# Moving the first head's load and two differential steps ahead of the end of the local units, with a fetch of local outputs moved forward

## The chip, the cores and the metric

The kernel runs on one core of one Trainium2 chip, in one launch. The metric is the device time of one execution in microseconds, taken as the median of several executions. The engines are named as in the profile: PE (TensorE), DVE (VectorE), ACT (ScalarE), POOL (GpSimd), SP (SyncE, which here only issues DMAs).

## The reference

One encoder layer with 1024 tokens and 16 meta tokens ahead of them, model width 1024, everything in float32. What is computed, cut to what matters here:

```python
h = h + 0.5 * swiglu(rmsnorm(h), ...)            # FFN 1
z = rmsnorm(h) @ w_in                            # one projection, columns split in groups
# group A: differential attention, 4 heads, 2 components of 64 dims each, full length 1040
s = einsum('bqhcd,bkhcd->bhcqk', q, k) * scale
p = softmax(s)
a = p[:, :, 0] - lam * p[:, :, 1]
A = rmsnorm(einsum('bhqk,bkhe->bqhe', a, v)) * (1 - lambda_init)
# group B: window attention +-128 tokens, 8 query heads on 2 key heads, a sink logit per head
B = softmax_with_sink(q . k in the band and the meta tokens) @ v
h = h + concat(A, rmsnorm(B)) @ w_out
h = h + 0.5 * swiglu(rmsnorm(h), ...)            # FFN 2
return rmsnorm(h)
```

## The kernel before, in words

Every product that needs float32 accuracy is made of several passes over numbers that are split in a high part (a rounding, on ACT) and a low part (the subtraction, L114). The layer runs in stages: FFN 1, the projections, attention, the output projection, FFN 2. The order of the instructions of each engine is settled at build time by a scheduler that simulates the program; each engine then takes its own instructions strictly in that order, and SP takes its DMA issues in order as well.

**Projections and local units.** The projections (`pj`, L167, and `pv`) go through DRAM: their outputs `z` get a rotary step (a product `zs` on POOL, two additions on DVE, L851) and are written to `qa_d`, `ka_d` (differential queries and keys), `qb_d`, `kb_d` (local ones). Beside them run the 16 *local units*, one for each of 2 key heads and 8 blocks of 128 queries. A unit consists of `win_keys`, `win_scores` (four products `ws`, for each a masked minimum on DVE, L1044, and an exponential on ACT, L1060; then `es`, `rz`, and four scalings on POOL, L1068) and `win_values` (four transposes `wt` for each key block, split in `thi` on ACT and `tlo` on DVE, and two products for each block into one accumulator `wo`, L1095; the result goes over `otmp` and `ow` to `ow_d`). The probabilities of a unit live in a ring `p4` of 4 buffers. `wo`, `otmp` and `ow` have one buffer each, so a unit's first `wo` product waits until DVE has added up the unit before.

The generator `fillers` is drawn from inside the local units: `qb_pair`, then `ka_pair`/`qa_pair` twice (the last projections), then `early_steps`, which loads the first differential head and makes the first N_EARLY of the differential steps.

**Differential steps.** There are 32 of them (4 heads, 8 query tiles). One step has two *score products* `ds` (components 0 and 1, six matmuls each, L780), for each a row minimum `dmx` on DVE (L784) and an exponential `dp` on ACT (L786), then `combine` (a reciprocal on DVE, L791, a scaling on POOL, L793, and a sum of both on DVE, L794). The combined tile is transposed (`wt` in the early steps, `dt` in the loop) and copied to `at` by DVE (L808) and ACT (L810, L814) two steps later. For each pair of steps `values` (L1228) multiplies with `v` and ACT copies the result to `oh`. Score products are counted below as S(step).(component), from S0.0 to S31.1.

**Loading a head.** `load_head` (L745) fetches `kraw` and `qraw` of a component with SP from `ka_d` and `qa_d`, ACT casts them to `kh` and `qst` and POOL subtracts for `kl` (L114) and for the lower half of `qst` (L760). `kraw` and `qraw` have one buffer each.

**The loop and its side work.** The main loop (L1243) starts at step N_EARLY = 4. `win_norm` is called at i = 4 and 8: it loads half of the local outputs from `ow_d` into `own` (L1171, one buffer), ACT and POOL make the sum of squares (L1148, L1151, L1152), PE sums over partitions (L1154), and POOL, ACT and DVE scale and split (L1174 to L1177) into `ow_hi`, `ow_lo`. From i = 9 on, odd steps draw from `out_fill`: the local half of the output projection (`out_win`, L1207, twelve matmuls `do<-ow_hi/ow_lo` for each of 16 pieces). What is left of it after the loop is run behind the loop.

## Time and profile before

| | us |
|---|---|
| three runs | 2072.01, 2071.40, 2064.84 |
| median | 2071.4 |
| the profiled execution: its own time | 2065.43 |
| its span in the trace | 2063.7 |
| last projection's matmul starts | 979.4 |
| last local product `wo` starts | 1061.0 |
| first product of the output projection starts | 1122.5 |
| S15.1, the 32nd score product, starts | 1159.9 |

Over the whole span PE is busy 94%, DVE 62%, ACT 43%, POOL 46%. The stage that the change touches lies between 979.4 and 1159.9 us. A row of the timeline gives start, busy time, engine, line, names and, in brackets, the idle time that lay just before it with the instruction that ended it. Starts of successive matmuls say more about PE than its busy time, since matmuls overlap.

### The profile page before, as it was taken

To read this page: it belongs to the slowest core of one execution; us is meant where nothing else is said; L and a number is where in the kernel's file an instruction comes from. 1 tells how busy PE (TensorE), PEld (TensorE's weight loads), DVE (VectorE), ACT (ScalarE), POOL (GpSimd) and SP (SyncE) were. 2 spreads that over 40 slices of the span, in tenths; PEclk is the share of its full clock that TensorE was granted. 3 is DMA by queue.
4 is the path that set the end of the run, shared out by engine and by line. 5 is a ranking of instruction groups with operands and counts; after the bars stand their busy time and mean duration, and the time that the engine had idled before them with its cause. 6 is when DMAs were issued, how large, how long until landed. Compare 5 with 4: busy or idle time off the path is not lost.

```text
span 2063.7 us, 30320 instructions
## 1 busy us (share of the span) xinstructions
PE 1942.7 (94%) x11484; PEld 1686.3 (82%) x11484; DVE 1281.4 (62%) x1857; ACT 880.0 (43%) x1630; POOL 950.8 (46%) x807
## 2 busy tenths in 40 slices
PE   5999999999999999999787999998999999989998
PEld 4999999998999889888555777676888888867777
DVE  7855555547874670277877777477655545587745
ACT  6433333334442441365766666353333333334433
POOL 0555554545443750666635433004655454454443
PEclk8999999999999999999898999999999999999999
DMA  4232323228522341533613322523323323475222
GB/s 173 99 118 99 119 83 109 88 100 314 169 70 77 127 147 62 132 104 80 152 49 87 98 67 72 179 92 96 123 103 113 107 77 123 147 265 164 62 82 82
DMA packets 104275, 237.82 MB, mean 115 GB/s; under 512 B 14016, under 2 KB 28816, under 8 KB 104128
## 3 DMA queue, kind: packets, MB, share of 16 engines
q1 hardware_dynamic: 92608, 198.20, 30.7%
q0 software_dynamic: 11520, 37.67, 4.7%
q8 instruction: 90, 1.47, 0.3%
q14 instruction: 57, 0.47, 0.1%
HBM read 169.86 MB, written 65.44 MB: 114 GB/s over the span
## 4 chain that ended last, share of the span: by engine, by line
PE 73%; DVE 11%; ACT 5%; DMA 5%; POOL 3%; issue 3%; SPq 1%; DVEq 0%; POOLq 0%; ACTq 0%
PE p L226 39%; PE pA L577 8%; PE pj L167 4%; PE pC L577 4%; PE pv L936 3%; PE do L1228 2%; PE pd L167 2%; PE ds L780 2%; PE po L167 2%; PE pB L577 2%; DVE bl L114 2%; PE do L167 1%; PE wo L1095 1%; ACT dp L786 1%; DMA wdraw<-wd 1%
## 5 line engine op out<-in xcount | busy, mean ns | idle before, releaser
L114 POOL TENSOR_TENSOR s<-ru 128x512 f32<-128x512 f32 x42 | 55.6, 1323 | 258.1 <-DMA ru<-wu 189.5
L226 PE MATMUL p<-b_hi,wal 128*128 128x260 f32 (+1 forms) x528 | 142.2, 324 | 5.1 <-DVE wal L114 5.1
L226 PE MATMUL p<-t_hi,wch 128*128 128x260 f32 (+1 forms) x528 | 140.8, 321 | 6.5 <-DVE u L114 6.5
L226 PE MATMUL p<-b_hi,wah 128*128 128x260 f32 (+1 forms) x528 | 143.6, 326 | 3.4 <-ACT sg L252 1.9
L226 PE MATMUL p<-b_lo,wah 128*128 128x260 f32 (+1 forms) x528 | 143.3, 324 | 3.3 <-DVE b_lo L114 3.3
L226 PE MATMUL p<-t_lo,wch 128*128 128x260 f32 (+1 forms) x528 | 140.6, 320 | 0.0
L226 PE MATMUL p<-t_hi,wcl 128*128 128x260 f32 (+1 forms) x528 | 140.2, 320 | 0.0
L226 PE MATMUL p<-t_lo,wbh 128*128 128x260 f32 (+1 forms) x504 | 135.9, 320 | 0.0
L114 DVE TENSOR_TENSOR u<-p,m 128x520 f32<-128x520 f32 (+1 forms) x88 | 60.9, 691 | 119.7 <-PE p L226 113.0
L226 PE MATMUL p<-t_hi,wbh 128*128 128x260 f32 (+1 forms) x504 | 133.4, 320 | 0.0
L226 PE MATMUL p<-t_hi,wbl 128*128 128x260 f32 (+1 forms) x504 | 133.3, 320 | 0.0
L117 ACT CAST wch<-ru 128x512 fp32r<-128x512 f32 x88 | 54.6, 621 | 153.8 <-PE p L226 80.0
L117 ACT CAST wbh<-s 128x512 fp32r<-128x512 f32 x84 | 52.1, 620 | 157.0 <-PE p L226 140.3
L577 PE MATMUL pA<-bh,wh 128*128 128x260 f32 (+1 forms) x432 | 116.0, 323 | 1.2 <-DVE h L584 1.2
L577 PE MATMUL pA<-bl,wh 128*128 128x260 f32 (+1 forms) x432 | 115.6, 321 | 0.0
L577 PE MATMUL pA<-bh,wl 128*128 128x260 f32 (+1 forms) x432 | 113.0, 322 | 1.6 <-POOL wl L114 1.6
L117 ACT CAST wah<-rg 128x512 fp32r<-128x512 f32 x88 | 53.9, 621 | 133.2 <-PE p L226 103.2
L114 DVE TENSOR_TENSOR bl<-r,bh 128x520 fp32r<-128x520 f32 (+1 forms) x126 | 107.5, 888 | 3.5 <-ACT bh L117 3.0
L584 DVE SCALAR_TENSOR_TENSOR h<-pA,h 128x520 f32<-128x520 f32 (+1 forms) x96 | 66.1, 690 | 65.7 <-PE pA L577 65.6
L117 ACT CAST wh<-s 128x384 fp32r<-128x384 f32 x96 | 49.0, 513 | 130.5 <-PE pA L577 64.4
L114 POOL TENSOR_TENSOR s<-wr 128x384 f32<-128x384 f32 x48 | 56.1, 1170 | 99.9 <-DVE wl L114 93.5
L226 PEld LDWEIGHTS p<-b_hi,wal 128*128 128x128 f32 x528 | 89.1, 192 | 14.0 <-DVE wal L114 6.2
(299 smaller groups left out, 6144.5 us busy)
## 6 DMA issues: line engine op xcount, KB each, us to landing
rg<-wg SPq DMA_DIRECT2D x44, 512.0 KB, 3.7
ru<-wu SPq DMA_DIRECT2D x44, 512.0 KB, 5.3
wr<-wd SPq DMA_DIRECT2D x24, 768.0 KB, 4.3
r<-g_t SPq DMA_DIRECT2D x12, 780.0 KB, 5.8
r<-g_t SPq DMA_DIRECT2D x12, 768.0 KB, 5.3
g_b<-g POOLq DMA_DIRECT2D x27, 260.0 KB, 5.2
r<-g_b SPq DMA_DIRECT2D x9, 780.0 KB, 5.5
g_b<-g POOLq DMA_DIRECT2D x27, 256.0 KB, 5.5
```

What stands on the lines that cost most here:

```text
L114: eng.tensor_tensor(out, a, b, op=op)
L117: nc.scalar.copy(hi, src)
L167: nc.tensor.matmul(o, w, x[:, c0 : c0 + n], start=first and i == 0, stop=last and i == 2)
L226: nc.tensor.matmul(o, w_k(ww, k), x[:, k, c0 : c0 + cn], start=first and k == 0 and i == 0, stop=k == hk - 1 and i == 2, skip_group_check= ...
L577: nc.tensor.matmul(o, w_k(ww, k), xx[:, c0 : c0 + cn], start=new and k == 0 and q == 0, stop=k == DNG - 1 and q == 2, skip_group_check=not ...
L584: nc.vector.scalar_tensor_tensor(hs, full, 0.5, hs, op0=ALU.mult, op1=ALU.add)
L780: nc.tensor.matmul(o, qs[c][:, qt * P : (qt + 1) * P], kk[:, c0 : c0 + n], start=i == 0, stop=i == 1)
L786: nc.scalar.activation(p, full, AF.Exp, bias=mx, scale=-1.0, accum_out=z[:, c : c + 1])
L936: nc.tensor.matmul(ps[:m, 192 + c * 320 : 512 + c * 320], u[:, k, sl], w[:, k, c * 320 : (c + 1) * 320], start=k == 0 and i == 0, stop=k = ...
L1095: nc.tensor.matmul(po, vb[:m, vt, kv, :], t[:m, :], start=j == 1 and i == 0, stop=j == nk + 1 and i == 1)
L1228: nc.tensor.matmul(po[:, :256], v[:m, j, :], at[:m, j, :], start=j == 0, stop=j == NB)
```

## The change

- N_EARLY goes from 4 to 6: two more steps are made inside `fillers`, and the loop begins at step 6. LOAD_GAP, the number of empty turns between the head's load and the first step, goes from 14 to 4.
- `kraw` and `qraw` of head 0, component 0, are fetched by `load_raw` into two buffers of the local pool (`hraw`) right behind the first `ka_pair`/`qa_pair`, while the second pair is still being projected. Component 1 is fetched where it was.
- The four subtractions for head 0 (`kl` and `qst` of both components) go from POOL to DVE. The other heads keep POOL.
- An early step now goes: score 0, `combine` of the step before, two of the three transposes of the step two before, score 1, the last transpose. Head 1 is loaded at early step 4, and the values of the first pair are made there, on the local score banks `ws`.
- The ring `p4` has 3 buffers instead of 4.
- The load of `own` is a function of its own, `win_load`: the first is issued ahead of the loop, the second right behind the first `win_norm` at i = 6; the second `win_norm` is at i = 9 (before: 4 and 8). `out_fill` starts at odd i above 9.

The diff, cut to its core:

```diff
-N_EARLY = 4
-LOAD_GAP = 14
+N_EARLY = 6
+LOAD_GAP = 4
...
+    def load_raw(hd, c, raw_tile):
+        row = (hd * 2 + c) * 64
+        raws = []
+        for tag, src, n in (("kraw", ka_d, L), ("qraw", qa_d, SEQ)):
+            t = raw_tile(tag)[:, :n]
+            for half in range(2):
+                nc.sync.dma_start(t[half * 64 : half * 64 + 64, :], src[row : row + 64, :])
+            raws.append(t)
+        return raws
+
+    def load_head(hd, ready=None, eng=None):
...
+            kraw, qraw = ready[c] if ready and c < len(ready) else load_raw(hd, c, lambda tag: kp.tile([P, L], F32, tag=tag, name=tag))
...
-            split(kh, kl, kraw, nc.gpsimd)
+            split(kh, kl, kraw, eng or nc.gpsimd)
             nc.scalar.copy(q, qraw)
-            nc.gpsimd.tensor_tensor(q[64:P, :], qraw[64:P, :], q[64:P, :].bitcast(F32), op=ALU.subtract)
+            tt(eng or nc.gpsimd, q[64:P, :], qraw[64:P, :], q[64:P, :].bitcast(F32), ALU.subtract)
...
             for p in range(2):
                 yield from ka_pair(p, nc.gpsimd)
                 yield from qa_pair(p, nc.gpsimd)
-            yield from early_steps()
+                ready = ready or [
+                    load_raw(0, 0, lambda tag: wp.tile([P, L], F32, tag="hraw", name=tag, bufs=2))
+                ]
+            yield from early_steps(ready)
...
-            heads[0] = load_head(0)
+            heads[0] = load_head(0, ready, nc.vector)
...
             for i in range(N_EARLY):
                 sc[i] = score_tiles()
-                for c in range(2):
-                    scores(heads[0], i, c, sc[i], ds)
-                    yield
+                scores(heads[0], i, 0, sc[i], ds)
                 if i:
                     pend[i - 1] = combine(*sc.pop(i - 1))
-                if i >= 2:
-                    yield from step_transposes(i, lambda: wps.tile([P, 512], F32, tag="wt", name="wt"))
+                yield
+                moves = step_t(i)
+                for _ in range(2):
+                    next(moves, None)
                     yield
+                scores(heads[0], i, 1, sc[i], ds)
+                yield
+                next(moves, None)
+                if i == 4:
+                    heads[1] = load_head(1)
+                if i >= 4 and i % 2 == 0:
+                    pr = (i - 4) // 2
+                    yield from values(
+                        heads[0], ats.pop(pr), ohs[0], pr, lambda: wps.tile([P, 512], F32, tag="ws", name="ws")
+                    )
...
-            p4 = wp.tile([P, 4, 400], F32, tag="p4", name="p4", bufs=4)
+            p4 = wp.tile([P, 4, 400], F32, tag="p4", name="p4", bufs=3)
...
+        win_load(0)
         for i in range(N_EARLY, NQ + 4):
...
-            elif i >= 9:
+            elif i > N_EARLY + 3:
                 work = fill
...
-            if i in (4, 8):
-                win_norm(i // 8)
+            if i == N_EARLY:
+                win_norm(0)
+                win_load(1)
+            if i == N_EARLY + 3:
+                win_norm(1)
```

What it does to the order of instructions, at four places. Names: `ws`, `wt`, `wo` belong to local units, `ds` to a differential score product, `pj` to the projections; the last part of a row is the shape, and "x4" means four such rows in a row.

On PE, where the first score product S0.0 stands. Before, it is the 31st row behind the last projection:

```order
L1040 MATMUL ws<-kxh,wqs 128x400
L1040 MATMUL ws<-kxl,wqs 128x400
L1084 MATMUL wt<-ident,p_11630 128x128 x4
L780 MATMUL ds<-kh,qst 128x264
L780 MATMUL ds<-kh,qst 128x512
L780 MATMUL ds<-kh,qst 128x264
```

Now it is the 14th:

```order
L1072 MATMUL ws<-kxh,wqs 128x400
L1072 MATMUL ws<-kxl,wqs 128x400
L1127 MATMUL wo<-thi,vb 128x512
L784 MATMUL ds<-kh,qst 128x264
L784 MATMUL ds<-kh,qst 128x512
```

Behind the last projection PE had 23 `ws` pairs, 34 `wo` pairs and 128 transposes of local work left; now it has 26, 37 and 136 left, so that much stood ahead of the projections' end and no longer does. Up to the last `wo` product it made 9 score products (S0.0 to S4.0) and now makes 11 (S0.0 to S5.0).

On DVE, the subtractions of component 1 of head 0, whose inputs come from DMAs that SP issues only behind the last projection. Before, they are on POOL, between scalings of local units:

```order
L1068 TENSOR_SCALAR p_12093<-p_12093,rz 128x400 x4
L114 TENSOR_TENSOR kxl<-kx,kxh 128x272
L114 TENSOR_TENSOR kl<-kraw,kh 128x1040
L760 TENSOR_TENSOR qst<-qraw,qst 64x1024
L1068 TENSOR_SCALAR p_12326<-p_12326,rz 128x400 x4
```

Now DVE has them:

```order
L114 TENSOR_TENSOR tlo<-wt,thi 16x512
L114 TENSOR_TENSOR kl<-kraw,kh 128x1040
L114 TENSOR_TENSOR qst<-qraw,qst 64x1024
L114 TENSOR_TENSOR z<-z,zs 128x1024
L1089 TENSOR_TENSOR es<-mx,nsink 128x4
L1135 TENSOR_TENSOR ow<-wo,otmp 64x512
```

So the addition `ow` that frees the one `wo` accumulator stands behind the two subtractions, and DVE takes them in order.

On PE, what stands ahead of the first product of the output projection. Before, it follows S11.1:

```order
L813 MATMUL dt<-ident,dp_13220 16x128
L805 MATMUL dt<-ident,dp_13273 128x128 x4
L780 MATMUL ds<-kh,qst 128x264
L780 MATMUL ds<-kh,qst 128x512
L780 MATMUL ds<-kh,qst 128x264
L780 MATMUL ds<-kl,qst 128x264
L780 MATMUL ds<-kl,qst 128x512
L780 MATMUL ds<-kl,qst 128x264
L167 MATMUL do<-ow_hi,owhi 128x512
```

Now it follows S14.0:

```order
L784 MATMUL ds<-kl,qst 128x264
L784 MATMUL ds<-kh,qst 128x264
L784 MATMUL ds<-kh,qst 128x512
L784 MATMUL ds<-kh,qst 128x264
L784 MATMUL ds<-kl,qst 128x264
L784 MATMUL ds<-kl,qst 128x512
L784 MATMUL ds<-kl,qst 128x264
L167 MATMUL do<-ow_hi,owhi 128x512
```

Between the last `wo` and that place stood 15 score products and now stand 18; from there to S15.1 stood 7 score products and 3 pieces of the output projection and now stand 2 and 2. From S15.1 on PE's rows are the same to the end of the loop, except that one more piece of the output projection is left for behind the loop.

On ACT, ahead of the second sum of squares of local outputs. Before, one exponential stands between the last `ow_hi` of the first half and it:

```order
L1176 ACTIVATE ow_hi<-own,wgain 128x512
L814 COPY at<-dt 16x128
L786 ACTIVATE dp_13220,dz<-ds,dmx_13218 128x1040
L1201 COPY nv<-do 128x512
L810 COPY at<-dt 128x4x128
L1148 ACTIVATE nacc<-own 128x512
```

Now:

```order
L1214 ACTIVATE ow_hi<-own,wgain 128x512 x3
L828 COPY oh<-do 128x256
L818 COPY at<-dt 16x128
L790 ACTIVATE dp_13332,dz<-ds,dmx_13330 128x1040
L814 COPY at<-dt 128x4x128
L790 ACTIVATE dp_13343,dz<-ds,dmx_13341 128x1040
L818 COPY at<-dt 16x128
L790 ACTIVATE dp_13406,dz<-ds,dmx_13404 128x1040
L1180 ACTIVATE nacc<-own 128x512
```

Three exponentials now stand between the two instead of one.

## Rows read from the trace of the kernel before

**Rows 1.** Busy us (and count) of PE, PEld, DVE, ACT, POOL by stretch, PE clock.

```profile
979.60:1061.40 81.80, 63.58 (x312) 45.20 (x311) 66.85 (x126) 56.52 (x124) 43.50 (x44) 0.90 0.48 113
1061.40:1122.50 61.10, 44.90 (x215) 33.23 (x214) 42.24 (x45) 42.95 (x73) 30.74 (x21) 0.91 0.26 76
1122.50:1159.90 37.40, 34.61 (x172) 27.07 (x171) 29.01 (x34) 23.39 (x40) 14.92 (x11) 0.97 0.23 71
```

**Rows 2.** PE timeline behind the last projection: start us, busy us, line, names, count.

```profile
979.59 0.34 PE L1040 MATMUL ws<-kxh,wqs 128*128 128x400 f32 x1
...
979.96 0.39 PE L1095 MATMUL wo<-thi,vb 128*128 128x512 f32 x1
980.19 0.35 PE L1040 MATMUL ws<-kxh,wqs 128*128 128x400 f32 x1
...
980.78 1.03 PE L1084 MATMUL wt<-ident,p 128*128 128x128 f32 x8
981.57 0.43 PE L1040 MATMUL ws<-kxh,wqs 128*128 128x400 f32 x1
```

**Rows 3.** Timeline of all engines at the first head's load; waits in brackets.

```profile
987.22 1.06 ACT L117 CAST kh<-kraw 128x1040 fp32r<-128x1040 f32 x1 [1.67 <-DMA kraw<-ka_d]
...
988.36 2.44 POOL L114 TENSOR_TENSOR kl<-kraw,kh 128x1040 fp32r<-128x1040 f32 x1 [2.91 <-ACT kh L117]
...
988.67 2.14 DVE L1065 TENSOR_TENSOR rz<-z,es 128x4 f32<-128x4 f32 x1
...
988.81 0.46 PE L1040 MATMUL ws<-kxh,wqs 128*128 128x400 f32 x1 [2.07 <-DVE mx L1044]
...
990.87 3.32 POOL L760 TENSOR_TENSOR qst<-qraw,qst 64x1024 fp32r<-64x1024 f32 x1
...
994.24 0.59 PE L780 MATMUL ds<-kh,qst 128*128 128x264 f32 x1 [0.47 <-POOL qst L760]
```

**Rows 4.** DVE groups, local stretch: busy us, mean ns, idle before and releasers.

```profile
L114 DVE TENSOR_TENSOR tlo<-wt,thi 128x512 fp32r<-128x512 f32 x24 | 16.2, 681 | 4.7 <-ACT thi L117 4.5
L1044 DVE CUSTOM_DVE_ANT_0 p<-ws,mask,nsink 128x400 f32<-128x400 f32 x19 | 11.5, 623 | 1.8 <-PE wt L1084 0.9 <-PE ws L1040 0.9
L784 DVE TENSOR_REDUCE dmx<-ds 128x1 f32<-128x1040 f32 x9 | 11.1, 1235 | 3.6 <-PE ds L780 2.7 <-DMA qa_d<-z 0.8
...
L1065 DVE TENSOR_TENSOR rz<-z,es 128x4 f32<-128x4 f32 x6 | 5.3, 877 | 0.0
L1057 DVE TENSOR_TENSOR es<-mx,nsink 128x4 f32<-128x4 f32 x6 | 4.5, 757 | 0.0
L794 DVE SCALAR_TENSOR_TENSOR dp<-dp,drz,dp 128x1040 f32<-128x1040 f32 x3 | 3.9, 1293 | 0.0
L114 DVE TENSOR_TENSOR z<-z,zs 128x1024 f32<-128x1024 f32 x2 | 2.4, 1210 | 0.0
...
L1066 DVE RECIPROCAL rz<-rz 128x4 f32<-128x4 f32 x6 | 1.0, 165 | 0.0
```

**Rows 5.** Timeline at the second load of the local outputs, all engines.

```profile
1097.38 0.58 SPq L1171 DMA_DIRECT2D own<-ow_d  x1
...
1103.10 0.38 PE L813 MATMUL dt<-ident,dp 128*16 128x128 f32 x1 [4.62 <-DVE at L808]
...
1103.16 0.63 ACT L1148 ACTIVATE nacc<-own 128x512 f32<-128x512 f32 x1 [8.12 <-DMA own<-ow_d]
```

**Rows 6.** PE timeline between the last local unit and the 32nd score product.

```profile
1149.11 0.48 PE L167 MATMUL do<-ow_hi,owhi 128*128 128x512 f32 x1
...
1151.94 0.27 PE L813 MATMUL dt<-ident,dp 128*16 128x128 f32 x1
...
1155.16 1.89 PE L1228 MATMUL do<-at,v 128*128 128x256 f32 x8
...
1159.88 0.74 PE L780 MATMUL ds<-kh,qst 128*128 128x264 f32 x3
```

**Rows 7.** ACT group of the local exponentials in the local stretch.

```profile
L1060 ACT ACTIVATE p<-p,mx 128x400 f32<-128x400 f32 x19 | 11.9, 628 | 3.5 <-DVE mx L1044 1.7 <-POOL p L1068 1.6
```

More of the change, by code (lines that the diff above doesn't have):

```diff
@@ L743, in layer @@
     kp = dp = None
-    def load_head(hd):
+    def load_raw(hd, c, raw_tile):
[8 more added lines that the diff above has]
+    def load_head(hd, ready=None, eng=None):
         khs, kls, qs = [], [], []
         for c in range(2):
-            row = (hd * 2 + c) * 64
-            kraw = kp.tile([P, L], F32, tag="kraw", name="kraw", bufs=1)
-            qraw = kp.tile([P, SEQ], F32, tag="qraw", name="qraw", bufs=1)
+            kraw, qraw = ready[c] if ready and c < len(ready) else load_raw(hd, c, lambda tag: kp.tile([P, L], F32, tag=tag, name=tag))
             kh = kp.tile([P, L], F32R, tag="kh", name="kh")
@@ L753, in load_head @@
             q = kp.tile([P, SEQ], F32R, tag="qst", name="qst")
-            for half in range(2):
-                hs = slice(half * 64, half * 64 + 64)
-                nc.sync.dma_start(kraw[hs, :], ka_d[row : row + 64, :])
-                nc.sync.dma_start(qraw[hs, :], qa_d[row : row + 64, :])
-            split(kh, kl, kraw, nc.gpsimd)
+            split(kh, kl, kraw, eng or nc.gpsimd)
             nc.scalar.copy(q, qraw)
-            nc.gpsimd.tensor_tensor(q[64:P, :], qraw[64:P, :], q[64:P, :].bitcast(F32), op=ALU.subtract)
+            tt(eng or nc.gpsimd, q[64:P, :], qraw[64:P, :], q[64:P, :].bitcast(F32), ALU.subtract)
             khs.append(kh)
@@ L814, in transposes, with values @@
         nc.scalar.copy(at[:NM, NB, qsl], pt[:NM, :P])
+    def values(head, at, oh, qc, po_tile):
+        v = head[3]
+        po = po_tile()
+        for j in range(NB + 1):
+            m = P if j < NB else NM
+            nc.tensor.matmul(po[:, :256], v[:m, j, :], at[:m, j, :], start=j == 0, stop=j == NB)
+            if j == 4:
+                yield
+        nc.scalar.copy(oh[:, qc * 256 : (qc + 1) * 256], po[:, :256])
+        yield
     def step_transposes(i, pt_tile):
@@ L983, in fillers @@
             yield from qb_pair(1, nc.gpsimd)
+            ready = None
             for p in range(2):
@@ L986, in fillers, with early_steps @@
                 yield from qa_pair(p, nc.gpsimd)
-            yield from early_steps()
-        def early_steps():
+                ready = ready or [
+                    load_raw(0, 0, lambda tag: wp.tile([P, L], F32, tag="hraw", name=tag, bufs=2))
+                ]
+            yield from early_steps(ready)
+        def early_steps(ready):
             nonlocal kp, dp
@@ L1166, in rsqrt, with win_load @@
             return r
+        owns = {}
+        def win_load(c):
+            c0, n = CH_REAL[c]
+            owns[c] = npool.tile([P, 4, 512], F32, tag="own", name="own")
+            nc.sync.dma_start(owns[c], ow_d[:, :, c0 : c0 + n])
         def win_norm(c):
             c0, n = CH_REAL[c]
-            ow = npool.tile([P, 4, 512], F32, tag="own", name="own")
-            nc.sync.dma_start(ow, ow_d[:, :, c0 : c0 + n])
+            ow = owns.pop(c)
             r = rsqrt(sums([ow[:, t, :] for t in range(4)], n), n, 512)
@@ L1221, in out_win @@
             yield
-        def values(head, at, oh, qc):
-            v = head[3]
-            po = psum.tile([P, 512], F32, tag="do", name="do")
-            for j in range(NB + 1):
-                m = P if j < NB else NM
-                nc.tensor.matmul(po[:, :256], v[:m, j, :], at[:m, j, :], start=j == 0, stop=j == NB)
-                if j == 4:
-                    yield
-            nc.scalar.copy(oh[:, qc * 256 : (qc + 1) * 256], po[:, :256])
-            yield
         def out_fill():
@@ L1268, in layer @@
                 hd2, qc = divmod(pr, 4)
-                work = values(heads[hd2], ats.pop(pr), ohs[hd2], qc)
-            elif i >= 9:
+                work = values(
+                    heads[hd2], ats.pop(pr), ohs[hd2], qc, lambda: psum.tile([P, 512], F32, tag="do", name="do")
+                )
+            elif i > N_EARLY + 3:
                 work = fill
```

4 lines of the change are left out of this document (added).

## The prediction

> **What bounds the kernel now.** I first read the table of windows, to find the stages in which PE, busy 94% over the whole span, is not the limit. Up to the last projection at 979.6 us PE has almost no gap, so whatever leaves that stage ends it earlier one for one. Behind it come three stretches with gaps [rows 1] (a row gives the stretch, its length, then the engines): the local stretch up to the last `wo` (81.8 us, PE busy 63.6, DVE 66.9), the middle up to the first output projection (61.1, PE 44.9, DVE 42.2) and the piece up to S15.1 (37.4, PE 34.6). PE, DVE, ACT and POOL all have gaps in the first two, so no engine bounds them by its work; chains through all four do. From S15.1 on the order on PE is the same in both kernels, so the question is how long the three stretches, 180.3 us together, take afterwards. What is moved is mostly not removed: the total of DVE and ACT work stays within 5 us. A gain can only come from gaps that get filled.
>
> Next I read the gaps. In the local stretch DVE is the busiest engine and idle for 81.8 − 66.9 = 15.0 us. The largest known hole is the load of the first head [rows 3]: ACT waits for `kraw` until 987.2, POOL subtracts `kl` and `qst` until 994.2, and S0.0 starts at 994.24, 14.6 us behind the last projection. During POOL's two subtractions DVE's tiny `rz` takes 2.14 us, and it ends when POOL's `kl` does. The middle has one hole: the second `own` is issued at 1097.38, and ACT stands still for 8.12 us in front of the sum of squares that needs it; the exponentials behind it in ACT's queue, and with them PE (4.62 us in one wait), wait too [rows 5].
>
> **The change part by part.** The sums are made against the profiled execution, 2065.43 us (span 2063.7); the median of the three runs, 2071.4, is 6.0 above it, so I carry the difference over to the median.
>
> (A) *End of the projections.* 3 `ws` pairs, 3 `wo` pairs and 8 transposes of local work no longer stand ahead of it. On PE, start to start, a `ws` pair takes 0.37, one `wo` product 0.23, eight transposes 0.79 [rows 2]: 3×0.37 + 6×0.23 + 0.79 = 3.3 us. PE has no gap there, so the end comes **3.3 earlier**. The two preloads add four DMA issues to SP, behind which weight loads are queued. They cost nothing as long as those weight loads are early; if not, each us of delay is a us on PE. I bound that by 0 and 3 us, the lead that is gained here.
>
> (B) *Local stretch*, counted as DVE work, since DVE has most of it. Prices from the DVE groups [rows 4].
> - Two score products more are finished in it: two minima at 1.24, one combining sum 1.29, its reciprocal (as the 0.165 of a 128x4 one), two copies to `at` (as a `tlo`, 0.68): 2.5 + 1.3 + 0.2 + 1.4 = +5.3.
> - Four subtractions of head 0 come to DVE. The trace has none there; the nearest row is the 128x1024 addition at 1.21, so 4 × 1.2 = +4.8.
> - The local work deferred in (A): 3 masked minima at 0.62 and 3 `tlo` at 0.68: +3.9.
> - Six `rz` and six `es` cost 5.3 + 4.5 = 9.8; at 0.165 each they would cost 2.0. The excess of 7.8 falls while POOL does its six subtractions for heads 0 and 1. Four of the six go, so I take back two thirds: −5.2.
> Together 66.9 + 8.8 = 75.7. Idle time: the 10.1 us of differential work and subtractions do not depend on the local units, so I let half of them fall into gaps; 15.0 − 5.0 leaves 10, and the stretch takes **85.7** (+3.9). Bounds: DVE nearly full at 95% gives 79.7; the density of before, 66.9/81.8 = 82%, gives 92.3. I choose between them because a new wait stands against the filling. Component 1 of head 0 is still fetched behind the last projection. By the row of component 0 before, `kh` can start 7.6 us behind it [rows 3]; cast and subtractions make it some 12 us. DVE waits in order, and behind its two subtractions stands the `ow` that frees the one `wo` accumulator, so PE's `wo` products stand still for what is left of the 12 us once their predecessors are done, at most about 6.
>
> Here a rule bears on the move to DVE. The Trainium skill, page "SBUF — State Buffer", section "Who interferes with whom", says that a DVE instruction with two inputs in SBUF and a GpSimd instruction that reads SBUF exclude each other for the whole instruction, whoever starts first. The trace agrees: `rz` at 2.14 us ends with POOL's `kl`. By that rule taking the subtractions off POOL helps `rz` and `es`, but the four subtractions on DVE have two SBUF inputs as well and can themselves be held behind POOL.
>
> (C) *Middle.* 15 score products in 61.1 us before; 18 now. Without the wait for `own` one takes (61.1 − 8.1)/15 = 3.53, so 18 take 63.6. The wait: two more exponentials now stand between the last reader of the first `own` and the first reader of the second, two turns of the loop at 3.53 = 7.1 of the 8.1 us are covered, 1.0 is left. The middle takes **64.6** (+3.5). Bounds: DVE's own work for one product, 42.2/15 = 2.8, gives 50.7; the pace with the whole stall, 4.07, gives 73.3. The loads of head 1 that now fall partly into (B) are not taken off, so the value leans to the slow side.
>
> (D) *From the first output product to S15.1.* One piece of the output projection takes 1151.94 − 1149.11 = 2.83, one `values` with its transposes 1159.88 − 1155.16 = 4.72 [rows 6]. Before, 3 pieces, 3 `values` and 7 score products took 37.4, so a score product here costs (37.4 − 8.5 − 14.2)/7 = 2.1, waits included. Now 2 pieces, 2 `values` and 2 products: 5.7 + 9.4 + 4.2 = **19.3** (−18.1).
>
> (E) One piece more is left behind the loop: **+2.8**; 0 if it fills a gap there.
>
> Sum: 85.7 + 64.6 + 19.3 = 169.6 against 180.3 is −10.7; with −3.3 and +2.8 it is **−11.2**: 2054.2 for the profiled execution, 2060.2 on the median.
>
> **The rivals.**
> *1. The work is only displaced.* In the local stretch all four engines already have a share, and a dense order of chains may fill no gap. At the density of before the stretch takes 92.3, +6.6: −4.6 in all, **2066.8**. For it: DVE's largest idle groups are waits for ACT's `thi` (4.5 of 4.7 us [rows 4]), and ACT gets more work as well. Against it: the 14.6 us until S0.0, which the preload shortens.
> *2. The collision changes sides.* Each of the four subtractions on DVE first waits for a POOL instruction that is under way, at the 2.44 us of a `kl` [rows 3]: +9.8, in all −1.4, **2070**. This is what the page's rule above would make of it if POOL always came first; the trace shows it for `rz` and `es`. Against it: a rotary product and one head's subtractions are all that POOL has left of that kind.
> *3. The gaps close.* The local stretch at 95% (79.7) and the middle halfway to DVE's own pace (57.7): −6.0 and −6.9 more, −24.1, **2047**. For it: the granted clock is only 0.90 and 0.91 there [rows 1], and it should rise with fewer gaps. Against it: no stretch behind the projections shows such a density.
> *4. Slower: the ring of three.* A local unit keeps its `p4` from the first `ws` to the last `wt`. Some 37/4.6 = 8 units are left in the stretch, about 10 us each, so a ring of four lets a unit take 40 us and a ring of three 30. The chain's own work is four minima (2.5), four exponentials (2.5), four scalings (about as long) and five splits (3.4), 11 us; the ring decides if queueing behind score products stretches that beyond 30. Then the next unit's minima wait for the scalings and transposes, and I price a turn at what it can no longer overlap, the 2.5 us of its exponentials [rows 7]: 8 × 2.5 = 20, **2080**. For it: ACT already waits 1.6 us for POOL's scaling [rows 7]. Against it: a factor of nearly three is needed.
> *5. The change does not do what it says.* The order shows that it does, with one exception: the second `own` has the same single buffer, so `win_load(1)` is early in the code, but the DMA can leave only when the first half is scaled. If ACT's extra exponentials come late for another reason, the stall stays and up to 7.1 us of (C) is lost: 2067, near rival 1, and counted there.
>
> **How the numbers follow.** A difference of 0.5%, 10.4 us, is about what a measurement of this kernel can tell from no change. Forecast 0.48 (2060, own range 2055 to 2066), rival 1 with 5 0.22, rival 2 0.07, rival 3 0.13, rival 4 0.10. The forecast lies just beyond 0.5%, so I give 0.29 of its 0.48 to faster and the rest to same; with rival 3 and a little of rival 1, faster is 0.45. Slower is rival 4 and the worst of rival 1, 0.12. Same is 0.43. The range leaves out half of rival 3 below and rival 4 above: 2047 to 2073.
>
> **What would show it.** Right: last projection near 976; S0.0 within 7 us of it and a wait of PE before a `wo` near 12 us behind it; the local stretch 80 to 92 us long with DVE idle about 10; `rz` and `es` mostly near 0.2 us; ACT's wait for `own` under 3 us; first output product behind S14.0 and 19 to 21 us from there to S15.1. Wrong: weight-load waits of the projections (A); a local stretch over 92 us with ACT or PE waiting for POOL's scaling, or `ws` for a free `p4` (rival 4); DVE subtractions of over 2 us (rival 2); ACT still waiting some 8 us for `own` (rival 5).

## The result and the profile after

The changed kernel is slower: 2080.5 us (median of 6 runs, 2075.8 to 2083.9) against 2069.4 us before, a ratio of 1.0056 with a 95% interval of 1.0042 to 1.0069, that is +11.6 us (+8.7 to +14.3). The forecast was 2060 with a range up to 2073. Executions of one kernel spread by some 10 us here, and the profiled one of before (2065.4) lies near the lower end; so costs below are ratios of the timed runs, multiplied by 2069, and the profiles, one for each kernel, serve to find the place.

The stretches of the changed kernel, split as in [rows 1] (length, then busy time and count of PE, PEld, DVE, ACT, POOL, then the granted PE clock):

```profile
976.50:1072.10 95.60, 77.50 (x378) 56.48 (x378) 78.82 (x151) 65.77 (x148) 36.84 (x42) 0.88 0.35 86
1072.10:1141.00 68.90, 54.29 (x234) 40.28 (x233) 50.92 (x52) 47.61 (x82) 43.06 (x26) 0.79 0.24 68
1141.00:1165.20 24.20, 19.22 (x91) 14.35 (x89) 14.02 (x19) 13.69 (x22) 6.36 (x5) 1.00 0.28 88
1165.20:1281.80 116.60, 108.97 (x586) 88.26 (x585) 87.75 (x101) 76.22 (x136) 46.90 (x31) 1.00 0.25 75
```

The landmarks of both profiles, in us:

| | before | after | difference | forecast |
|---|---|---|---|---|
| last projection starts | 979.4 | 976.3 | −3.1 | −3.3 |
| from it to the last `wo` | 81.7 | 95.5 | +13.8 | +3.9 |
| from there to S15.1 | 98.9 | 93.5 | −5.4 | −14.6 |
| from S15.1 to the first product of FFN 2 | 199.7 | 207.1 | +7.4 | +2.8 |
| FFN 2 to the end of the span | 704.1 | 701.4 | −2.7 | 0 |
| span | 2063.7 | 2073.7 | +10.0 | −11.2 |

FFN 2 is not touched, and takes 701 to 707 us in all kernels shown here; −2.7 is spread. What lies ahead spreads as well: the first `ws` product starts between 845.1 and 851.7 us. From that product to the first one of FFN 2, with both spreads left out, it takes 511.8 us before and 523.6 after, +11.8. The three rows in the middle are what has to be explained: the local stretch grew by 10 us more than forecast, what was taken out behind it gave back 9 us less, and 4.6 us more came at the end of attention.

DVE's groups in the local stretch, to be read against [rows 4] (busy us, mean ns, idle before with its releasers):

```profile
L1076 DVE CUSTOM_DVE_ANT_0 p<-ws,mask,nsink 128x400 f32<-128x400 f32 x24 | 14.4, 622 | 7.4 <-PE wt L1116 6.8 <-PE ws L1072 0.6
L788 DVE TENSOR_REDUCE dmx<-ds 128x1 f32<-128x1040 f32 x11 | 13.5, 1229 | 1.8 <-PE ds L784 1.8
...
L1097 DVE TENSOR_TENSOR rz<-z,es 128x4 f32<-128x4 f32 x7 | 3.8, 546 | 1.7 <-ACT es L1090 1.7
L114 DVE TENSOR_TENSOR kl<-kraw,kh 128x1040 fp32r<-128x1040 f32 x2 | 2.5, 1261 | 0.0
L114 DVE TENSOR_TENSOR qst<-qraw,qst 64x1024 fp32r<-64x1024 f32 x2 | 2.4, 1222 | 0.1
...
L1089 DVE TENSOR_TENSOR es<-mx,nsink 128x4 f32<-128x4 f32 x7 | 1.4, 204 | 0.1
```

The subtractions on DVE take 1.26 and 1.22 us, as priced, and `rz` and `es` fell from 877 and 757 ns to 546 and 204. New is what the first row shows: before, the masked minima waited 0.9 us for transposes, now 6.8 us. A minimum writes into a `p4` buffer, so it has to wait until the transposes `wt` have read the unit that had the buffer before. DVE is idle for 95.6 − 78.8 = 16.8 us; before it was 15.0, and 10 were forecast. No gap was filled. PE says the same: by the rows above and [rows 1] it is idle for 95.6 − 77.5 = 18.1 us, and before for 81.8 − 63.6 = 18.2.

### The profile page after: what moved, and what is told of

It is laid out like the page before. It is cut to its first block, busy times and chain, and to the rows that moved or that the text cites. A ratio compares the mean times of both kernels' runs of the same rounds, so it can differ in the third digit from the quotient of the medians.

```text
span 2073.7 us, 30316 instructions
## 1 busy us (share of the span) xinstructions
PE 1947.9 (94%) x11484; PEld 1689.1 (81%) x11484; DVE 1282.2 (62%) x1861; ACT 879.8 (42%) x1630; POOL 943.6 (46%) x803
## 4 chain that ended last, share of the span: by engine, by line
PE 74%; DVE 12%; ACT 5%; DMA 4%; issue 3%; POOL 2%; SPq 0%; DVEq 0%; POOLq 0%; ACTq 0%
PE p L226 38%; PE pA L577 8%; PE pj L167 5%; PE pC L577 4%; PE pv L951 3%; PE pd L167 2%; DVE bl L114 2%; PE ds L784 2%; PE po L167 2%; PE pB L577 2%; PE do L825 2%; PE do L167 1%; PE wo L1127 1%; ACT dp L790 1%; PE wt L1116 1%
## 5 line engine op out<-in xcount | busy, mean ns | idle before, releaser
L117 ACT CAST wh<-s 128x384 fp32r<-128x384 f32 x96 | 49.0, 513 | 131.1 <-PE pA L577 67.5
L114 DVE TENSOR_TENSOR wal<-rg,wah 128x512 fp32r<-128x512 f32 x88 | 71.0, 813 | 53.9 <-ACT wah L117 52.5
L114 POOL TENSOR_TENSOR s<-wr 128x384 f32<-128x384 f32 x48 | 55.7, 1162 | 101.7 <-DVE wl L114 93.5
```

The source lines that it names most:

```text
L114: eng.tensor_tensor(out, a, b, op=op)
L117: nc.scalar.copy(hi, src)
```

## The experiments

Each kernel was timed beside the kernel before on one chip. "Local" is the time from the last projection to the last `wo` with the score products that start in it; "behind" is the time from the last `wo` to FFN 2, with the products up to S15.1 and the pieces of the output projection up to there (both from the profile; the expectations count S15.1 itself as well, so one product more).

| label | edit | us against before (95%) | local: us, products | behind: us, products, pieces |
|---|---|---|---|---|
| (before) | | 0 | 81.7, 9 | 298.6, 22, 3 |
| (after) | the change | +11.6 (8.7 to 14.3) | 95.5, 11 | 300.6, 20, 2 |
| b_p3 | ring of 3 alone | +8.3 (4.8 to 11.8) | 88.8, 9 | 303.9, 22, 3 |
| a_nopre | change, no preload | +13.4 (10.6 to 16.6) | 98.5, 11 | 298.0, 20, 2 |
| a_nopre_p4 | change, no preload, ring of 4 | +11.2 (7.4 to 14.9) | 93.4, 11 | 302.0, 20, 2 |
| a_fill9 | change, output pieces from i = 9 | +13.0 (9.7 to 16.1) | 95.7, 11 | 300.5, 20, 2 |
| b_dve | DVE subtractions alone | +1.9 (−1.2 to 5.2) | 81.6, 9 | 302.4, 22, 3 |
| a_pool | change, subtractions on POOL | +13.2 (8.9 to 17.6) | 96.1, 11 | 298.0, 20, 2 |
| b_gap4 | short gap alone | +2.3 (−0.4 to 4.8) | 88.6, 11 | 301.7, 20, 3 |
| a_e4_nopre_p4 | a_nopre_p4 with 4 early steps | +7.4 (4.8 to 9.9) | 85.8, 10 | 304.2, 21, 3 |
| b_order | order of an early step alone | −4.1 (−6.6 to −1.4) | 76.8, 7 | 301.9, 24, 3 |
| b_norm47 | second norm at 7 alone | +6.6 (3.7 to 9.5) | 82.1, 9 | 307.1, 22, 3 |
| b_gap22 | longer gap | −3.3 (−6.4 to −0.4) | 76.6, 7 | 302.2, 24, 3 |
| b_e2 | 2 early steps | −11.0 (−14.7 to −7.2) | 74.3, 6 | 297.7, 25, 3 |
| a_n10 | change, second norm at 10 | +8.1 (5.0 to 11.4) | 97.5, 11 | 299.1, 20, 2 |
| b_e6 | 6 early steps alone | +7.4 (5.0 to 10.1) | 81.9, 9 | 306.7, 22, 2 |
| b_e3 | 3 early steps | −0.6 (−3.3 to 1.9) | 83.6, 9 | 298.6, 22, 3 |
| b_e2_order | 2 early steps, new order | −7.9 (−11.4 to −4.3) | 75.6, 6 | 297.4, 25, 3 |
| b_skip3 | 3 products left out | −5.0 (−7.9 to −2.1) | 80.5, 9 | 298.3, 19, 3 |
| b_own5q | `own` in quarters | +7.7 (5.0 to 10.1) | 81.5, 9 | 308.9, 22, 3 |

The theories at the start: the ring of three slows the local units; or the work that DVE got in the local stretch is paid in full; and the sixth piece behind the last score product costs more than its matmuls.

**The ring.** b_p3:

```diff
-p4 = wp.tile([P, 4, 400], F32, tag="p4", name="p4", bufs=4)
+p4 = wp.tile([P, 4, 400], F32, tag="p4", name="p4", bufs=3)
```

> The kernel before with one edit: the ring p4 has 3 buffers instead of 4. Nothing else is changed. Theory 'ring': the ring lets fewer local units overlap, so 3 pairs and 8 transposes are left behind the last projection (26, 37, 136 instead of 23, 34, 128 by the order), DVE's masked minima wait for transposes that free a buffer (6.8 us in the changed kernel, 0.9 before), and the local stretch gets longer by more than the 3.1 us that the projections end earlier: the stretch 81.7 -> 89 to 93 us, the whole kernel 4 to 9 us slower than before. Theory 'vector work' (the ring is harmless, the extra work on DVE in the local stretch costs): within 3 us of before, the stretch not over 85 us.

Slower by 8.3 us, of which the interval leaves at least 4.8. Its local stretch, and what DVE waited for in it:

```profile
977.30:1066.20 88.90, 71.16 (x332) 49.82 (x332) 69.57 (x140) 61.72 (x138) 45.43 (x45) 0.87 0.42 104
```

```profile
DVE dmx L784 <- PE ds L780: 7.4, 5, 2.8
DVE p L1044 <- PE wt L1084: 5.6, 3, 4.4
```

The stretch is 7.1 us longer, and 5.6 us of waiting for `wt` stand where 0.9 stood: what the ring theory said comes true. But not all of the 7.1 us is new. From the first `ws` to the last projection it takes 127.5 to 127.8 us in the six kernels with a ring of 3, and 131.1 to 131.6 in the fourteen with 4. Some 3.9 us of local work are only put off past the projections, so term (A) of the prediction is no gain by itself, and up to the last `wo` the ring alone costs 7.1 − 3.9 = 3.2 us. The rest of the 8.3 lies behind the last `wo` (303.9 for 298.6 us), with the same products and pieces; why is not shown. PE is not idle longer in the stretch (17.7 us for 18.2), but busy longer: 332 matmuls for 312, at a granted clock of 0.87 for 0.90.

The other pair undoes the preload (`ready` stays None), and then gives the ring its fourth buffer back.

> The changed kernel without the preload: component 0 of head 0 is fetched behind the last projection, as before; the ring p4 stays at 3. If the preload brings what its place suggests (S0.0 at 5.9 instead of 14.9 us behind the last projection), this is 3 to 6 us slower than the changed kernel. If only component 1 counts (the first step is combined when both are there), within 2 us of it.

> The changed kernel without the preload and with the ring p4 at 4 (the two do not fit together: the preload's two buffers take the room of the fourth). Against the run without the preload and with 3 buffers it isolates the ring once more, in the changed order. Theory 'ring': 5 to 10 us faster than that run, local stretch 8 us shorter or more, projections' end 3 us later. Theory 'vector work': within 3 us of it.

Without the preload the change costs 13.4, with it 11.6; the intervals overlap, so what the preload brings is not clear of noise. With S0.0 at 5.9 instead of 14.2 us behind the last projection it does what it says. The ring's part between a_nopre and a_nopre_p4 is 2.2 us with wide intervals, less than the 5 to 10 expected. The traces agree with so little up to the last `wo`: with the fourth buffer the local stretch is 5.1 us shorter and the projections end 3.0 later, 2.1 us in all.

**The subtractions.** b_dve gives head 0's `split` and `qst` to DVE; a_pool takes them back in the changed kernel (`heads[0] = load_head(0, ready)`).

> The kernel before with one edit: the four subtractions of head 0 are on DVE instead of POOL. Theory 'dense DVE' (the local stretch keeps its 15 to 20 us of DVE idle time, so DVE work that is added there is paid in full): 4.8 us of DVE work more, some 5 us of inflated rz and es less, so the stretch stays at 80 to 84 us and the kernel within 3 us of before. Theory 'collision changes sides': each subtraction waits for a POOL instruction, 2.4 us each; stretch 90 us or more, kernel 6 to 10 us slower.

> The changed kernel with the four subtractions of head 0 on POOL again. Theory 'dense DVE': 4.8 us of DVE work less, rz and es inflated again: within 3 us of the changed kernel. If the addition ow standing behind component 1's subtractions on DVE (PE waited 3.25 us for it) is what costs: 3 us or more faster.

Neither shows that their place matters: +1.9 with zero inside the interval, and 13.2 against 11.6, also within the noise. The wait that the prediction saw is there, 15.6 us behind the last projection, and 3.25 us long (PE timeline of the changed kernel):

```profile
982.18 0.74 PE L784 MATMUL ds<-kh,qst 128*128 128x264 f32 x3 [1.60 <-DVE qst L114]
...
991.90 0.79 PE L1127 MATMUL wo<-thi,vb 16*128 16x512 f32 x1 [3.25 <-DVE ow L1135]
```

**How much stands in the local stretch.** b_gap4 and b_gap22 set LOAD_GAP to 4 and 22, b_e2, b_e3 and b_e6 set N_EARLY to 2, 3 and 6, b_order has the new order of an early step.

> The kernel before with LOAD_GAP 4 instead of 14: by the order 11 instead of 9 score products stand ahead of the last local product, with the ring at 4, four early steps, and 5 pieces of the output projection behind the last score product as before. It moves two score products into the local stretch and nothing else. Theory 'dense DVE': the stretch grows by the full price of what comes in (5 to 6 us for each product, 10 to 12 in all, as in the run without preload with the ring at 4), the middle gives back 3.5 to 4.1 for each product, so the kernel is 2 to 6 us slower. Forecast of the prediction (half of it falls into gaps): stretch +4 to +6, kernel 2 to 5 us faster.

> The kernel before with one edit: the order inside an early step is that of the change (score 0, combining of the step before, two transposes, score 1, last transpose). The run with four early steps, no preload and the ring at 4 was 7.4 us slower than before; of its four parts the short gap gave +2.3 and the DVE subtractions +0.9 by themselves, so some 4 us are left for this order and for the earlier second norm. If it is the order: 3 to 6 us slower than before. If it is the norm: within 2 us of before. By the order of instructions 7 score products instead of 9 stand ahead of the last local product.

> The kernel before with LOAD_GAP 22 instead of 14: the opposite of the change. By the order of instructions 7 instead of 9 score products stand ahead of the last local product. Theory 'dense DVE' (work in the local stretch is paid in full, and in the middle as well, so it hardly matters where it stands): stretch 4 to 8 us shorter, middle longer by as much, the kernel within 3 us of before. Theory 'the local stretch is overfull': 3 us or more faster than before.

> The kernel before with two early steps instead of four: 6 instead of 9 score products ahead of the last local product. Theory 'dense DVE': within 3 us of before, the stretch some 10 us shorter and the middle longer by as much. Theory 'overfull': 3 us or more faster. Theory of the prediction (score products fill gaps of the local stretch): 5 us or more slower, since three of them lose their cover.

> The kernel before with three early steps: a point between two (11 us faster) and four. By the order 9 score products stand ahead of the last local product, as with four. If the number of early steps counts: 4 to 7 us faster than before. If the number of score products in the local stretch counts: within 3 us of before.

> The kernel before with six early steps instead of four (the values of the first pair and the load of head 1 therefore in them, the norms at 6 and 10, four steps apart as before); ring, gap, order of a step and subtractions as before. With two early steps the kernel was 11 us faster than before. If more early steps cost more: 4 to 11 us slower than before. If what matters is only how many score products stand ahead of the last local product (9 here as before, by the order): within 3 us of before.

> The kernel before with two early steps and the changed order inside an early step (4 us faster by itself): the one part of the change that gained, together with the opposite of the part that cost. If the gains add: 13 to 17 us faster than before, the fastest of all. With two early steps there is less for the order to act on: at least as fast as with two steps alone, 9 to 12 us faster than before.

> The changed kernel with four early steps instead of six, without the preload and with the ring at 4: what is left of the change is the order inside an early step, the short gap, the DVE subtractions and the later norms. By the order 10 score products stand ahead of the last local product and 5 pieces of the output projection behind the last score product (6 with six early steps). Theory 'tail': from the last score product to FFN 2 it takes 84 us instead of 93, and the kernel is 6 to 9 us faster than the run with six steps, no preload and the ring at 4. If pieces only change places and cost about the same anywhere: within 3 us of that run.

In the table, with a ring of 4, the local stretch takes 74.3 and 75.6 us with 6 score products in it, 76.6 and 76.8 with 7, 80.5 to 83.6 with 9, 85.8 with 10, 88.6 with 11 (93.4 with the DVE subtractions and the first values in it as well). That is (88.6 − 75.0)/5 = 2.7 us for each product, with its minimum, exponential and transposes. PE's idle time in the stretch lies between 15.7 and 18.7 us in all twenty kernels, while the stretch goes from 74.3 to 98.5 us: what is added is added to PE's busy time, and no product falls into a gap. Behind the last `wo` hardly anything is given back: the time to FFN 2 is 297 to 304 us with 20, 21, 22, 24 or 25 products, in all kernels but three (307 to 309): b_norm47 and b_own5q, which touch the norms, and b_e6. b_e2 shows it best (its three stretches, split as above):

```profile
977.90:1052.40 74.50, 58.04 (x284) 40.92 (x283) 62.05 (x120) 51.95 (x115) 41.27 (x42) 0.91 0.53 124
1052.40:1113.20 60.80, 48.25 (x237) 37.83 (x236) 45.06 (x52) 46.11 (x80) 36.95 (x23) 0.90 0.27 77
1113.20:1150.80 37.60, 35.39 (x177) 27.61 (x175) 27.80 (x34) 24.34 (x42) 15.53 (x12) 0.97 0.22 71
```

Three products fewer in the first stretch make it 7.4 us shorter, and three more behind it do not make that longer: 60.8 and 37.6 against 61.1 and 37.4 before [rows 1]. There they do fall into gaps: from the last `wo` to S15.1 PE makes 415 matmuls instead of 387 and is idle for 14.8 us instead of 19.0. With that the kernel is 11.0 us faster than before, the fastest at the median; it beats both kernels. The new order by itself gains 4.1 us and the longer gap 3.3, which fits the count (7 products); beside two early steps the new order adds nothing. On the other side the step from 9 to 11 products (b_gap4) makes the stretch 6.9 us longer, but the timed runs show only +2.3 (−0.4 to 4.8). b_e3, with 9 products in the stretch, is as fast as before. b_e6 is not explained by the count: it too has 9, and is 7.4 us slower. There the norms come at 6 and 10, and only 2 pieces of the output projection stand ahead of S15.1. a_e4_nopre_p4 fits neither of its theories: the tail from the last score product to FFN 2 is as short as forecast (84.6 us for 92.9), but the run is only 3.8 us faster than a_nopre_p4, which the intervals do not tell from nothing.

**The middle.** b_norm47 calls the second norm one step earlier than before; a_n10 calls it one step later than the change does (`N_EARLY + 4`). The edit of b_norm47:

```diff
-            if i in (4, 8):
-                win_norm(i // 8)
+            if i in (4, 7):
+                win_norm(i // 7)
```

> The kernel before with one edit: the second norm of the local outputs is called at i = 7 instead of 8, where the change has it relative to its first one. If the remaining 4 us of the run with four early steps, no preload and the ring at 4 are the norm's: 3 to 6 us slower. If they are the order's: within 2 us of before.

> The changed kernel with one edit: the second norm of the local outputs is called at i = 10 instead of 9, four steps behind the first one as before the change instead of three. In the kernel before, moving it from four steps to three (8 to 7) cost 6.6 us. If that holds in the changed kernel too: 4 to 9 us faster than the changed kernel, with DVE's ow_lo of the first norm no longer beside POOL's kl (6.3 us for three of them in the changed kernel, 0.74 each alone). If the two costs do not add: within 3 us of the changed kernel. By the order one piece less is not gained: 6 pieces stay behind the last score product.

A second norm that follows three steps behind the first costs 6.6 us alone, and one step more takes the changed kernel from +11.6 to +8.1 (2080.5 to 2077.0 at the medians; not clear of noise). Part of the cause in b_norm47 can be seen on ACT: the second `own` is still issued 37.5 us behind the first, so ACT meets it too early and waits 9.5 instead of 8.1 us [rows 5]. From the last `wo` to S15.1 PE is idle 5.5 us longer than before (24.5 for 19.0), and its 387 matmuls take 85.5 us at a granted clock of 0.88 instead of 80.0 at 0.93.

```profile
1101.38 0.63 ACT L1148 ACTIVATE nacc<-own 128x512 f32<-128x512 f32 x1 [9.53 <-DMA own<-ow_d]
```

b_skip3 takes three score products out of the stretch behind the local units; b_own5q takes away the reason for the wait for `own`:

```diff
-            ow = npool.tile([P, 4, 512], F32, tag="own", name="own")
-            nc.sync.dma_start(ow, ow_d[:, :, c0 : c0 + n])
+            ow = [npool.tile([P, 512], F32, tag="own", name="own", bufs=5) for _ in range(4)]
+            for t in range(4):
+                nc.sync.dma_start(ow[t], ow_d[:, t, c0 : c0 + n])
```

> The kernel before with three score products left out behind the local units: the second component of steps 7, 8 and 9 (its six matmuls, row minimum and exponential, and the sum of both components) is not computed, and the first one is scaled alone. 20 instead of 23 score products then stand between the last local product and S15.1, all else in its place. Theory 'fixed middle' (from the last local product to S15.1 it took 98.8 us with 23 score products and 98.8 with 26, so the chain of the local outputs' norms sets this time and the score products ride along): 96 to 101 us again, the kernel within 4 us of before. Theory of the prediction (a score product costs its share, (98.8 - 8.1)/23 = 3.9 us): 11 to 12 us shorter and the kernel 9 to 12 us faster.

> The kernel before with the local outputs loaded in quarters into a ring of five quarter buffers (before: one buffer of four quarters), so that a quarter of the second half can be loaded as soon as one buffer is free; same work and same norms at 4 and 8. This takes away the cause of ACT's 8.1 us in front of the second sum of squares. Theory 'fixed middle', the chain of the norms: that wait falls under 3 us, from the last local product to S15.1 it takes 93 to 96 instead of 98.8 us, the kernel 3 to 6 us faster. If the score products' pace sets the middle: the wait falls as well, but the kernel stays within 2 us of before.

b_skip3 refutes the prediction's rate. From the last `wo` to S15.1 it took 99.5 us with 19 products (98.9 with 22), as "fixed middle" has it; the timed runs are 5.0 us faster (2.1 to 7.9, where that theory allowed 4), 1.7 for each product, less than half of the 3.9 that the prediction's rate gives. So a product there costs something, but far less than its share. b_own5q does not bring the gain that "fixed middle" expected. The wait for `own` is gone, and the kernel is 7.7 us slower:

```profile
1095.64 0.61 ACT L1151 ACTIVATE nsq<-own 128x512 f32<-128x512 f32 x1
...
1097.88 0.62 ACT L1148 ACTIVATE nacc<-own 128x512 f32<-128x512 f32 x1
...
1105.32 1.06 ACT L117 CAST kh<-kraw 128x1040 fp32r<-128x1040 f32 x1 [6.34 <-DMA kraw<-ka_d]
...
1108.96 1.04 ACT L759 CAST qst<-qraw 128x1024 fp32r<-128x1024 f32 x1 [2.05 <-DMA qraw<-qa_d]
```

```profile
1091.54 8.41 SPq L1172 DMA_DIRECT2D own<-ow_d  x3
```

ACT's second sum of squares starts at 1095.64 without a wait, but three quarter loads now occupy SP for 8.4 us while they wait for their buffers, the next head's `kraw` is issued behind them, and ACT stands 6.34 and 2.05 us for it. The stall was passed on to the next transfer in SP's queue, so this run does not show what the middle is without one. Most of what the middle loses is matmul time: the same 387 matmuls take 6.6 us longer at a granted clock of 0.85 instead of 0.93, and PE is idle only 1.6 us longer (last `wo` to S15.1, before and b_own5q, columns as above).

```profile
1061.00:1160.00 99.00, 80.01 (x387) 60.72 (x386) 71.53 (x79) 66.35 (x114) 45.88 (x33) 0.93 0.25 74
1062.40:1169.60 107.20, 86.64 (x387) 65.68 (x385) 72.97 (x80) 66.07 (x113) 46.86 (x32) 0.85 0.22 64
```

**The tail.**

```diff
-            elif i > N_EARLY + 3:
+            elif i >= 9:
```

> The changed kernel with one edit: the output projection's pieces are drawn from odd i of 9 on, as before, instead of above 9. By the order one piece less (5 instead of 6) is left behind the last score product. Theory 'tail': the sixth piece costs far more there than its 2.83 us of matmuls, since the last head's sum of squares stands behind it on PE and the last products behind that; this run is 5 to 9 us faster than the changed kernel, and from the last score product to the last piece it takes 40 us as before instead of 47.9. Rival (the piece costs its own time only): 0 to 3 us faster.

The expected gain did not come (+13.0 against +11.6). From the last score product to FFN 2 it does take 83.3 us instead of 90.5, so the price of the sixth piece is right there; but from the last `wo` to the last score product it takes 217.2 instead of 210.1. The piece that was moved forward is paid where it went.

The early fetch itself needs no run: with the load put back into `win_norm`, the order of instructions is the same on every engine, in the changed kernel as in the one before. This part of the change moves nothing; only the norms' places do. The reason is the single buffer: in both kernels the second load leaves 0.03 us behind the last `ow_lo` that reads the first half (1097.35 to 1097.38 us before, 1109.44 to 1109.47 after).

## Where the prediction was right and where it was wrong

- *(A), the projections' end.* Right: −3.1 for −3.3, and −4.1 from the first `ws` on, without the spread of what lies ahead. What the term left out is the cause. It is the ring that puts this work off, and (B) had to pay more for it than (A) gained.
- *(B), the local stretch.* The step that failed: 95.5 us for 85.7, over the upper bound of 92.3. Two terms were mis-sized. The work put off by the ring was priced as DVE work, 3.9 us; the ring costs 7.1 in the stretch (b_p3). And half of the differential work was let fall into gaps; two products cost 2 × 2.7 = 5.4, all of it. 81.7 + 7.1 + 5.4 = 94.2 comes close to 95.5, in part by luck: it leaves out the rest of the change (+4.8 from b_gap4 to a_nopre_p4) and the preload (−3.0 from a_nopre to the changed kernel), which nearly cancel. The DVE sum itself (75.7) was near the 78.8 measured, and the subtractions cost nothing that is clear of noise. The error was to count an engine's gaps as room: of DVE's 15.0 us 5.0 were to be filled, and 16.8 are left. That these gaps are waits inside the chain of a local unit, over a ring, one `wo` accumulator and three engines, which a score product makes longer, is the likely reason; no run separates it.
- *(C), the middle.* Wrong in its rule. It took time in proportion to the score products (3.53 each); over 13 kernels with three pieces the time from the last `wo` to S15.1 lies between 98.0 and 110.0 without any trend from 25 products down to 19. The wait for `own` went away as forecast (0.36 us), and that gave nothing: the middle took 68.8 instead of 64.6 us, inside the bounds of 50.7 and 73.3, and the run that took the wait away by other means lost as well. PE's idle time in the middle did fall, from 16.2 to 14.6 us; what the term had no place for is the clock. PE was busy 54.3 us with 234 matmuls at a granted clock of 0.79; at the pace of before (44.9 us for 215, at 0.91) I estimate 48.9.
- *(D) and (E).* 24.7 for 19.3, and +7.4 for +2.8. In (D) PE was busy for 19.2 of 24.2 us; the 5 us of waits are what the price lacked. The sixth piece is not 2.83 us of matmuls: from the last score product to FFN 2 five kernels with six pieces take 89.8 to 93.0 us, the others with five 81.2 to 85.6. In the changed kernel PE is busy 3.9 us longer there than before (79.8 for 76.0) and idle 3.1 longer (10.7 for 7.6). A piece has its split and its addition to `hrm` too, and among PE's waits there are some for these (changed kernel, PE timeline behind the last score product):

```profile
1308.41 0.50 PE L167 MATMUL do<-ow_hi,owhi 128*128 128x512 f32 x1 [0.46 <-ACT oh L828]
...
1312.30 1.10 PE L1186 MATMUL do<-nacc,ones 128*128 128x512 f32 x2 [0.88 <-DVE hrm L114]
1315.56 0.80 PE L167 MATMUL do<-ow_hi,owhi 128*128 128x512 f32 x1 [2.17 <-DVE nt L1196]
...
1322.07 0.50 PE L167 MATMUL do<-ow_hi,owhi 128*128 128x512 f32 x1 [0.74 <-DVE hrm L114]
...
1330.95 0.47 PE L167 MATMUL po<-o_hi,owhi 128*128 128x512 f32 x1 [0.88 <-DVE hrm L114]
```

- *The rivals.* Rival 4, with a chance of 0.10, gave the time, 2080, and named the ring with the right sign in the trace (minima waiting for transposes). Its price was not right: 20 us for the ring alone, where the ring measures 8.3. That the sum came out at 2080 is luck: the 20 us stood on top of a gain of 11.2 that did not come. Rival 1, work that is only displaced, is what happened to the score products, more strongly than I put it: paid in full where they went, hardly repaid where they left. Rival 2 did not happen where it was expected (subtractions of 1.2 us), nor did rivals 3 and 5.
- *What stays open.* Single edits sum to +22.4 (ring 8.3, gap 2.3, subtractions 1.9, order −4.1, norm 6.6, six steps 7.4), twice what the change costs. They overlap, and which of them the changed kernel really pays cannot be told: no part of it that was undone brought back the time of before (the nearest are a_e4_nopre_p4, +7.4, and a_n10, +8.1), and the ring alone, undone beside a_nopre, gave 2.2. Nor is it settled what holds the time behind the last `wo` near 300 us: not the number of score products alone, and not the wait for `own` by itself. The granted clock has a part in it, as b_own5q and b_norm47 show.

## What to carry to other kernels

Before moving work from one stretch to another, find out from two or three variants whether the first one gets shorter when work leaves it; a stretch in which no engine is full can still be long for other reasons, and then the work is paid where it goes and not given back where it left. Do not count an engine's idle time inside a ring of buffers as room: look who waits for the ring, and price a buffer given away by a run of its own. A wait that is taken away at an in-order queue is only gone if what stands behind it in the queue was ready.

## What the runs showed of the hardware

A collision that I had looked for in the local stretch stands in the middle. Three DVE instructions `ow_lo`, with two inputs from SBUF, take 0.73 us each alone and 6.33 together while POOL subtracts `kl` and `qst` (timelines of DVE and POOL in the changed kernel, then ACT and PE):

```profile
1100.20 0.73 DVE L1215 SCALAR_TENSOR_TENSOR ow_lo<-own,wgain,ow_hi 128x512 fp32r<-128x512 f32 x1
...
1103.11 6.33 DVE L1215 SCALAR_TENSOR_TENSOR ow_lo<-own,wgain,ow_hi 128x512 fp32r<-128x512 f32 x3 [0.45 <-ACT ow_hi L1214]
```

```profile
1103.25 2.88 POOL L114 TENSOR_TENSOR kl<-kraw,kh 128x1040 fp32r<-128x1040 f32 x1
1106.21 2.68 POOL L114 TENSOR_TENSOR qst<-qraw,qst 64x1024 fp32r<-64x1024 f32 x1
```

```profile
1110.62 1.13 ACT L790 ACTIVATE dp<-ds,dmx 128x1040 f32<-128x1040 f32 x1 [4.34 <-DVE dmx L788]
...
1115.97 0.63 ACT L1180 ACTIVATE nacc<-own 128x512 f32<-128x512 f32 x1 [0.36 <-DMA own<-ow_d]
```

```profile
1111.89 1.24 PE L784 MATMUL ds<-kh,qst 128*128 128x264 f32 x3 [4.36 <-ACT dp L790]
```

DVE's row minimum comes behind them, ACT's exponential waits 4.34 us for it and PE 4.36 for that. The Trainium skill, page "SBUF — State Buffer", section "Who interferes with whom", describes this exclusion of two-input DVE instructions and reading GpSimd instructions, and the trace agrees; POOL's two instructions take 2.88 and 2.68 us, and DVE's third ends 0.55 us behind them. The prediction had looked for this beside head 0 [rows 3]. It is not what the change costs, though. Before, POOL's `kl` and `qst` hold up an `ow_lo` and a sum of both components (1.29 us elsewhere in [rows 4]) just as long:

```profile
1089.84 2.87 DVE L1177 SCALAR_TENSOR_TENSOR ow_lo<-own,wgain,ow_hi 128x512 fp32r<-128x512 f32 x1
1092.63 3.39 DVE L794 SCALAR_TENSOR_TENSOR dp<-dp,drz,dp 128x1040 f32<-128x1040 f32 x1
```

a_n10 was expected to pull the two apart and did not: there the three `ow_lo` take 6.35 us. In a_nopre none takes over 1.86 us, and that kernel is no faster (+13.4).

Behind the wait PE's clock is lower (windows of 10 us, columns as above):

```profile
1102.00:1112.00 10.00, 4.63 (x26) 3.04 (x25) 9.05 (x7) 5.50 (x12) 8.33 (x5) 0.93 0.21 52
1112.00:1122.00 10.00, 8.46 (x28) 6.17 (x28) 7.48 (x10) 4.98 (x10) 5.92 (x4) 0.50 0.59 160
```

After a window with PE busy 4.63 of 10 us the granted clock is 0.50, that is 1.2 of 2.4 GHz, and matmuls of a score product take 1.24 us for three where they take 0.74 otherwise. Over the middle the granted clock was 0.79 instead of 0.91. The collision alone does not explain that: a_nopre has 0.81 there without it.
